# Token-major projections of 512 columns in a hybrid encoder block, two heads' pairs of keys and queries by way of DRAM

## The chip, the core and the metric

The kernel runs on one NeuronCore of a Trainium2 chip. The metric is device time in microseconds (us), lowest is best; the median of three runs stands for a kernel. One further execution was taken by the hardware profiler, and all views below come from it. Engines are called as in the profile: PE (matrix multiply; PEld is its weight load), DVE (vector), ACT (scalar, activations), POOL (GpSimd) and SP (which here only issues DMAs).

## What is computed

One layer of an encoder on 1024 tokens of 1024 channels, in float32. Cut to what matters:

```
h = rmsnorm(x);  z = h @ w_in                      # 7176 columns, split as
hq, hf, hi, hg (512 each), fq, fk, fv (512 each), ff (8), mq (512), gate_logits (3072) = split(z)
y_a = hgrn2(hq, hf, hi, hg)                        # gated recurrence, 4 heads, 128 x 128 state; hi are its values
y_b = fox(fq, fk, fv, ff)                          # 8 heads x 64, per head:
      q, k = rmsnorm(fq), rmsnorm(fk)              #   over the 64 channels of the head
      p = softmax(q k^T / 8 + F_t - F_s, causal);  y = p v
y_c = memory_attention(mq, mem)
x  = x + (sum over branches of sigmoid(gate) * (y @ w_br)) @ w_out
x  = x + (gelu(conv3(h2 @ w_a)) * (h2 @ w_v)) @ w_down,   h2 = rmsnorm(x)
```

The change touches three pieces of the first line's product: `hi`, and `fk`, `fq` of heads 4 to 7.

## The kernel before

**Three matmuls for one product.** Every float32 operand is split into a high part (rounded to the PE's fast format) and a low part (the rest). `mm3` (lines 158 to 162) multiplies high by high, high by low and low by high into one PSUM tile. A weight piece arrives by DMA in a `raw` tile (two buffers), ACT casts it into `wh` (L166), DVE subtracts to get `wl` (L174); `wh` and `wl` have three buffers each of 4 x 264 columns (`weights`, lines 188 to 198). All of this is in SBUF for `uh` and `ul`, the two parts of the normalised input, 8 chunks of 128 channels by 1024 tokens.

**Two ways to project.** `cm_chunk` (lines 200 to 217) makes a channel-major result: the weights stand in the PE, 512 tokens stream through, 2 x 8 x 3 = 48 matmuls of 512 columns for 128 channels. `token_major` (lines 704 to 715) makes a token-major one: a 128-token block of `uh`/`ul` stands in the PE, the weight columns stream. It is called with 256 columns (264 for the second half of attention's values): two weight pieces of 4 x 256, then for each of 8 token blocks 8 x 3 = 24 matmuls into one PSUM tile of the ring `pp` (three buffers), which an `evac` on ACT scales by the token's norm `rt` and copies out.

**Fill and attention.** The FoX attention (`fox_attn`, lines 901 to 972) is done in halves (p, i), pair of heads p = 0..3, head i of the pair. For each of 8 query blocks: scores on PE (L924, L925), bias and maximum on DVE (L930), exponential on ACT (L940), scaling on POOL (L942); for each two blocks transposes on PE (L953, L954), a split, products with the values (L965, L966), and a DMA to `ybd` (L971). As this chain leaves PE time over, `weave` (lines 97 to 106) emits it together with fill, and a scheduler that simulates the engines sets the order on each engine, attention's instructions with their priority moved 300 ahead. The order on each engine's queue is then fixed, DMA issues on SP included.

The fill of each half, before: `fox_proj(p + 1)` (lines 844 to 864: keys and queries of the next pair, 256 columns, 8 tiles) in (0,0), (1,0), (2,0); three gate chunks (`gates_early`, 48 matmuls of 512 columns and two results to DRAM each) in (0,1), (1,1), (2,1); eight tiles of `hgrn_values` (lines 1012 to 1016) and one gate chunk in (3,0), the other eight tiles in (3,1). `NFOX` deals the gate chunks. `fox_proj`'s evac writes tiles `z` of four token blocks (two buffers) and after each fourth block normalises them: a square on ACT (L859, into a buffer of the ring `pt`, which attention's probabilities share), a sum on DVE (L860), a power on POOL (L179), a multiplication on DVE (L862). `fox_prep(p + 1)` (lines 866 to 892) then transposes `z` on PE (L878), after the last score matmul of half (p, 0), and builds the operands of pair p + 1, which is used one half later. Behind attention comes the recurrence: `hgrn_prep` (six results of 48 / 2 matmuls a head) is its fill, `hgrn_mix` its chain.

Unrelated to that, POOL issues DMAs by software (`G.dma_start`): weights of the dense units and of the second half's channel mixer, and the sums of the down weights.

Of the kernel before, what the change touches and what calls it, by code (L numbers as in the profile page):

```python
# [8 lines left out]
F32 = mybir.dt.float32  # L9
F32R = mybir.dt.float32r  # L10
# [4 lines left out]
P = 128  # L15
T = 1024
D = 1024
KC = D // P
# [9 lines left out]
ORDER = [(br, j) for br in (1, 0, 2) for j in range(8)]  # L28
NCOVER, NPAIR = 2, 10
NDULL = 8  # L30
NFOX = [0, 3, 0, 3, 0, 3, 1]

_dense = [12, 13, 14, 15] + [16 + 8 * br + j for br, j in ORDER[4:4 + NPAIR]]
PAIRS = list(zip(_dense[0::2], _dense[1::2]))
assert 2 + NCOVER + NPAIR + sum(NFOX) == len(ORDER) and len(_dense) % 2 == 0
# [56 lines left out]
def run_all(gen):  # L92
    for _ in gen:
        pass


def weave(*parts):

    live = [[g, max(n, 1), s[0] if s else 0.0, 0] for g, n, *s in parts]
    while live:  # L100
        p = min(live, key=lambda q: q[2] + (1.0 - q[2]) * q[3] / q[1])
        try:
            next(p[0])
            p[3] += 1
        except StopIteration:
            live.remove(p)


@with_exitstack
def tile_block(ctx: ExitStack, tc: tile.TileContext, xT, memT, x_rows, mem_rows, vec, fbias, mats, hmask, w_first, w_cm, w_hi, w_fqk, w_fv,  # L110
               w_mkv, w_br, w_out, w_up, w_dn, w_pair, outT):
    nc = tc.nc
    V, S, G, PE, SP = nc.vector, nc.scalar, nc.gpsimd, nc.tensor, nc.sync
# [34 lines left out]
    def ahead(gen, offset):  # L148

        while True:  # L150
            with tc.high_priority(offset) if offset else nullcontext():
                try:
                    next(gen)
                except StopIteration:
                    return
            yield

    def mm3(ps, lh, ll, rh, rl, first, last, more=False):

        PE.matmul(ps, lh, rh, start=first, stop=False, skip_group_check=more)  # L160
        PE.matmul(ps, lh, rl, start=False, stop=False, skip_group_check=more)  # L161
        return PE.matmul(ps, ll, rh, start=False, stop=last, skip_group_check=more)  # L162
# [259 lines left out]
    def first_weights(k):  # L422
        k0, k1 = WFIRST[k]
        if k % 4 == 0:
            gw[k // 4] = [wp.tile([P, 4 * 264], F32R, tag=t, name=t, bufs=3) for t in ("wh", "wl")]
# [133 lines left out]
    class Dense:  # L559
# [15 lines left out]

        def operand(self, src):
            if self.half is None:
                self.half = [wp.tile([P, 4 * 264], F32R, tag=t, name=t, bufs=3) for t in ("wh", "wl")]
# [137 lines left out]

# [124 lines left out]
    fox_sets = {}  # L841
    fox_z = {}

    def fox_proj(p):

        fox_z[p] = [None, None]

        def evac(tb, ps):
            n, b = tb // 4, tb % 4
            if b == 0:  # L850
                fox_z[p][n] = pq.tile([P, 4, 256], F32, tag="z", name=f"z{p}_{n}", bufs=2)
            z = fox_z[p][n]
            S.activation(z[:, b, :], ps, AF.Copy, scale=rt[:, tb:tb + 1])
            if b == 3:
                zz = z.rearrange("p b (h d) -> p (b h) d", d=64)
                sq = pools["pf"].tile([P, 16, 64], F32, tag="pt", name="fsq", bufs=4) if p else \
                    pm.tile([P, 16, 64], F32, tag="fsq", name="fsq")
                r = cp.tile([P, 16], F32, tag="fr", name="fr", bufs=2)
                S.activation(sq, zz, AF.Square)  # L859
                V.reduce_sum(r, sq, axis=AX.X)  # L860
                rstd_small(r, r, 64)
                V.tensor_mul(zz, zz, r.unsqueeze(2).to_broadcast([P, 16, 64]))  # L862
# [115 lines left out]
    mskf = pf.tile([P, P], F32, tag="mskf", name="mskf")  # L978
    SP.dma_start(mskf, mats[:, 2 * P:3 * P])
    fox_prep(0)  # L980
    for p in range(3):
        weave((ahead(fox_attn(p, 0), AHEAD), FOX_STEPS), (fox_proj(p + 1), 8))
        fox_prep(p + 1, fox_sets[p][3])
        weave((ahead(fox_attn(p, 1), AHEAD), FOX_STEPS), (gates_early(NFOX[2 * p + 1]), 2 * NFOX[2 * p + 1], FOX_LATE))


    state = {}
# [22 lines left out]
        SP.dma_start(state["rs"], mats[:, 3 * P:3 * P + HB])  # L1010

    def hgrn_values():
        for pc in range(2):
            def evac(tb, ps, pc=pc):
                S.activation(Vf[:, tb, pc * 256:(pc + 1) * 256], ps, AF.Copy, scale=rt[:, tb:tb + 1])
            yield from token_major(w_hi[pc], 256, evac)

    hset = {}

# [333 lines left out]
    def first_operands():  # L1353

        raw = []
        for i in range(2):
            t = wp.tile([P, 4 * 264], F32, tag="raw", name="raw", bufs=2)
            SP.dma_start(t[:, :2 * HB], w_up[0][:, 2 * i:2 * i + 2, :])
            raw += [t[:, :HB], t[:, HB:2 * HB]]
        a11, a21, a22, a12 = raw  # L1360
        h = [wp.tile([P, 4 * 264], F32R, tag="wh", name="wh", bufs=3) for _ in range(2)]
        sums = [wp.tile([P, 4 * 264], F32R, tag="wl", name="sums", bufs=3).bitcast(F32) for _ in range(2)]
# [346 lines left out]
def _layout(inp):  # L1709
# [68 lines left out]
    o["w_hi"] = c(np.stack(pieces(hi, [(0, 256), (256, 512)])))  # L1778
    o["w_fqk"] = c(np.stack([pieces(np.concatenate([fk[:, p * P:(p + 1) * P], fq[:, p * P:(p + 1) * P]], axis=1),
                                    [(0, 256)])[0] for p in range(4)]))  # L1780
# [34 lines left out]
```

## Time and profile before

| | us |
|---|---|
| runs | 1698.50, 1698.43, 1699.84; median 1698.5 |
| the profiled execution, its own time | 1700.23 |
| its span, first to last instruction | 1698.4 |
| PE busy | 1691.0 |
| DVE, ACT, POOL busy | 1150.8, 800.9, 324.6 |
| mean granted PE clock | 0.999 |

The span is what lies between the first and the last instruction of the program on the core; the execution's own time has 1.8 us more around it. A busy time is the union of the instructions' durations on an engine, so matmuls that overlap in the PE's pipeline count once. A row of a group has the line, the engine, the operation, the names written and read, shapes and count; then busy time, the mean duration of one in ns, and the engine's idle time before them. A line is often a helper's, so names tell more: `pp<-wh,uh 128x256` is token-major, `pp<-uh,wh 128x512` channel-major.

### The profile page before, as it was taken

To read this page: it belongs to the slowest core of one execution; us is meant where nothing else is said; L and a number is where in the kernel's file an instruction comes from. 1 tells how busy PE (TensorE), PEld (TensorE's weight loads), DVE (VectorE), ACT (ScalarE), POOL (GpSimd) and SP (SyncE) were. 2 spreads that over 40 slices of the span, in tenths; PEclk is the share of its full clock that TensorE was granted. 3 is DMA by queue.
4 is the path that set the end of the run, shared out by engine and by line. 5 is a ranking of instruction groups with operands and counts; after the bars stand their busy time and mean duration, and the time that the engine had idled before them with its cause. 6 is when DMAs were issued, how large, how long until landed. Compare 5 with 4: busy or idle time off the path is not lost.

```text
span 1698.4 us, 24291 instructions
## 1 busy us (share of the span) xinstructions
PE 1691.0 (100%) x8957; PEld 1452.4 (86%) x8957; DVE 1150.8 (68%) x2057; ACT 800.9 (47%) x1428; POOL 324.6 (19%) x420
## 2 busy tenths in 40 slices
PE   9999999999999999999999999999999999999999
PEld 7888899989898998888888888888888888888887
DVE  6966455666666664886856845987878888775654
ACT  6734455545454553775631333644434444533432
POOL 0200032543433331544310000311111111100000
PEclk9999999999999999999999999999999999999999
DMA  9443232221212111110346542566544344494772
GB/s 367 157 161 106 88 139 68 77 92 51 94 59 77 63 46 57 67 32 13 106 127 209 167 186 100 165 174 169 158 139 138 118 149 143 172 363 145 251 269 87
DMA packets 83062, 227.16 MB, mean 134 GB/s; under 512 B 9712, under 2 KB 12408, under 8 KB 82816
## 3 DMA queue, kind: packets, MB, share of 16 engines
q1 hardware_dynamic: 64320, 160.54, 26.8%
q0 software_dynamic: 18048, 64.50, 13.2%
q8 instruction: 70, 1.15, 0.3%
q10 hardware_dynamic: 576, 0.59, 0.1%
q14 instruction: 48, 0.39, 0.1%
HBM read 180.72 MB, written 67.93 MB: 146 GB/s over the span
## 4 chain that ended last, share of the span: by engine, by line
PE 99%; DVE 0%; ACT 0%; DMA 0%; issue 0%; ACTq 0%; DVEq 0%
PE pp L160 21%; PE pp L162 21%; PE pp L161 21%; PE lg L160 4%; PE lg L162 4%; PE lg L161 4%; PE tr L162 3%; PE tr L161 3%; PE tr L160 3%; PE po L966 1%; PE lg L925 1%; PE lg L924 1%; PE po L965 1%; PE po L160 1%; PE po L161 1%; PE po L162 1%
## 5 line engine op out<-in xcount | busy, mean ns | idle before, releaser
L160 PE MATMUL pp<-uh,wh 128*128 128x512 f32 x412 | 163.3, 396 | 0.0
L161 PE MATMUL pp<-ul,wh 128*128 128x512 f32 x412 | 162.9, 395 | 0.0
L162 PE MATMUL pp<-uh,wl 128*128 128x512 f32 x412 | 162.5, 394 | 0.0
L161 PE MATMUL pp<-wl,uh 128*128 128x256 f32 (+1 forms) x512 | 146.3, 286 | 0.0
L162 PE MATMUL pp<-wh,ul 128*128 128x256 f32 (+1 forms) x512 | 146.1, 286 | 0.0
L160 PE MATMUL pp<-wh,uh 128*128 128x256 f32 (+1 forms) x512 | 145.6, 286 | 0.0
L166 ACT CAST wh<-s 128x512 fp32r<-128x512 f32 x110 | 66.5, 621 | 131.6 <-PE pp L161 55.1
L166 ACT CAST wh<-raw 128x1024 fp32r<-128x1024 f32 (+2 forms) x76 | 67.6, 890 | 100.6 <-PE pp L161 86.2
L166 ACT CAST wh<-rw 128x512 fp32r<-128x512 f32 x87 | 53.2, 619 | 108.1 <-PE pp L161 70.2
L160 PEld LDWEIGHTS pp<-wh,uh 128*128 128x128 f32 x512 | 97.3, 190 | 1.2
L161 PEld LDWEIGHTS pp<-wl,uh 128*128 128x128 f32 x512 | 97.4, 190 | 1.0
L162 PEld LDWEIGHTS pp<-wh,ul 128*128 128x128 f32 x512 | 97.4, 190 | 0.9
L1457 POOL DMA_DIRECT2D rw<-in_w_up x44 | 24.1, 555 | 372.4 <-DVE wl L1350 171.3
L166 ACT CAST dwh<-wr 128x1024 fp32r<-128x1024 f32 (+1 forms) x41 | 40.2, 980 | 115.8 <-PE tr L161 40.0
L162 PEld LDWEIGHTS pp<-uh,wl 128*128 128x128 f32 x412 | 77.5, 188 | 15.1
L174 DVE TENSOR_TENSOR wl<-raw,wh 128x1024 fp32r<-128x1024 f32 (+2 forms) x75 | 78.0, 1040 | 17.8 <-ACT wh L166 17.6
L160 PEld LDWEIGHTS pp<-uh,wh 128*128 128x128 f32 x412 | 77.5, 188 | 14.6
L161 PEld LDWEIGHTS pp<-ul,wh 128*128 128x128 f32 x412 | 77.5, 188 | 14.5
L940 ACT ACTIVATE pt<-pt,st 128x128 f32<-128x128 f32 (+3 forms) x64 | 49.7, 777 | 41.7 <-DVE st L937 33.9
L174 DVE TENSOR_TENSOR dwl<-wr,dwh 128x1024 fp32r<-128x1024 f32 (+1 forms) x41 | 46.3, 1129 | 31.7 <-ACT dwh L166 31.7
L942 POOL TENSOR_SCALAR pt<-pt,st 128x128 f32<-128x128 f32 (+3 forms) x64 | 49.1, 767 | 78.4 <-DVE st L941 64.1
L1350 DVE TENSOR_TENSOR wl<-rw,wh 128x512 fp32r<-128x512 f32 x69 | 47.7, 704 | 22.7 <-PE pp L162 18.2
(500 smaller groups left out, 5123.2 us busy)
## 6 DMA issues: line engine op xcount, KB each, us to landing
rw<-in_w_up POOLq DMA_DIRECT2D x44, 512.0 KB, 4.7
sd<-in_w_dn POOLq DMA_DIRECT2D x30, 512.0 KB, 6.0
br<-yd SPq DMA_DIRECT2D x30, 512.0 KB, 5.0
raw<-in_w_cm SPq DMA_DIRECT2D x24, 512.0 KB, 3.4
gd<-gt SPq DMA_DIRECT2D x48, 256.0 KB, 2.0
gt<-gd SPq DMA_DIRECT2D x48, 256.0 KB, 2.7
yd<-fc SPq DMA_DIRECT2D x44, 256.0 KB, 2.2
wr<-sd SPq DMA_DIRECT2D x20, 512.0 KB, 4.5
```

What stands on the lines that cost most here:

```text
L160: PE.matmul(ps, lh, rh, start=first, stop=False, skip_group_check=more)
L161: PE.matmul(ps, lh, rl, start=False, stop=False, skip_group_check=more)
L162: return PE.matmul(ps, ll, rh, start=False, stop=last, skip_group_check=more)
L166: return S.copy(out, in_)
L174: return (sub or V).tensor_sub(l, src, h.bitcast(F32))
L924: PE.matmul(ps[:, :w], qa[i][:, tsl], kh[i][:, s0:s0 + w], start=True, stop=False)
L925: fox_sets[p][3] = PE.matmul(ps[:, :w], qa[i][:, tsl], kl[i][:, s0:s0 + w], start=False, stop=True)
L940: S.activation(pt[:, :ns], pt[:, :ns], AF.Exp, bias=st[:, 2:3], accum_out=st[:, 3:4])
L942: G.tensor_scalar(pt[:, :ns], pt[:, :ns], st[:, 3:4], 0.0, ALU.mult, ALU.add)
L965: PE.matmul(o, vhl[:, sb, :], ph[:, src], start=(sb == 0), stop=False)
L1350: late["split"] = V.tensor_sub(l, src, h.bitcast(F32))
L1457: late["raw"] = G.dma_start(raw[:, 2 * i:2 * i + 2, :], src[:, 2 * i:2 * i + 2, :])
```

## The change

The weights of `hi`, and those of `fk`, `fq` of pairs 2 and 3 together, become two arrays of 512 columns, `w_late`, in four pieces of 2 x 512 each; `token_major` takes two 128-row chunks a piece at 512 columns, four at 256 or 264. `hgrn_values` makes 8 tiles of 512 columns in place of 16 of 256. Pairs 2 and 3 are projected by `fox_proj_late`, 8 tiles of 512 columns, which go from a gate tile to the DRAM tile `zd`; `fox_load(p)` reads a pair's 256 columns back into `z` (two DMAs of four token blocks) and normalises. `wh` and `wl` get four buffers (`WIDE`), and the SBUF scratch of the software DMAs shrinks from its default of 16384 bytes a partition to 4096. The fill is dealt thus: (0,0) `fox_proj(1)`; (0,1) a gate chunk, then four late tiles; (1,0) four late tiles, with `fox_load(2)`; (1,1) three gate chunks; (2,0) two gate chunks, with `fox_load(3)`; (2,1) three; (3,0) one, then four tiles of the recurrence's values; (3,1) the other four.

```diff
-NFOX = [0, 3, 0, 3, 0, 3, 1]
+NFOX = 10
+WIDE = 4
@@ weights(), first_weights(), Dense.operand(), first_operands()
-            hl = [wp.tile([P, 4 * 264], F32R, tag=t, name=t, bufs=3) for t in ("wh", "wl")]
+            hl = [wp.tile([P, 4 * 264], F32R, tag=t, name=t, bufs=WIDE) for t in ("wh", "wl")]
@@ token_major()
-            w = [weights(src[q], (4, ncol)) for q in range(2)]
+            per = 2 if ncol == HB else 4
+            w = [weights(src[q], (per, ncol)) for q in range(KC // per)]
...
-                wh, wl = w[k // 4]
-                mm3(ps, uh[k][:, tsl], ul[k][:, tsl], wh[:, k % 4, :], wl[:, k % 4, :], k == 0, k == KC - 1)
+                wh, wl = w[k // per]
+                mm3(ps, uh[k][:, tsl], ul[k][:, tsl], wh[:, k % per, :], wl[:, k % per, :], k == 0, k == KC - 1)
@@
+    zd = tc.dram_tile([8, P, HB], F32, name="zd")
+
+    def fox_norm(p, z):
...
+    def fox_proj_late():
+
+        def evac(tb, ps):
+            t = gate_tile()
+            S.activation(t, ps, AF.Copy, scale=rt[:, tb:tb + 1])
+            SP.dma_start(zd[tb], t)
+
+        yield from token_major(w_late[0], HB, evac)
+
+    def fox_load(p):
+        cs = slice((p - 2) * 256, (p - 1) * 256)
+        for n in range(2):
+            z = fox_tile(p, n)
+            SP.dma_start(z, zd[4 * n:4 * n + 4, :, cs].rearrange("b p c -> p b c"))
+            fox_norm(p, z)
+            yield
@@
+    late_proj = fox_proj_late()
+    first = (fox_proj(1), islice(late_proj, 4), gates_early(2))
+    second = (chain(gates_early(1), islice(late_proj, 4)), gates_early(3), gates_early(3))
     for p in range(3):
-        weave((ahead(fox_attn(p, 0), AHEAD), FOX_STEPS), (fox_proj(p + 1), 8))
+        weave((ahead(fox_attn(p, 0), AHEAD), FOX_STEPS), (first[p], (8, 4, 4)[p]),
+              *([(fox_load(p + 1), 2, 0.5)] if p else []))
         fox_prep(p + 1, fox_sets[p][3])
-        weave((ahead(fox_attn(p, 1), AHEAD), FOX_STEPS), (gates_early(NFOX[2 * p + 1]), 2 * NFOX[2 * p + 1], FOX_LATE))
+        weave((ahead(fox_attn(p, 1), AHEAD), FOX_STEPS), (second[p], 6, FOX_LATE))
+    run_all(late_proj)
@@ hgrn_values()
-        for pc in range(2):
-            def evac(tb, ps, pc=pc):
-                S.activation(Vf[:, tb, pc * 256:(pc + 1) * 256], ps, AF.Copy, scale=rt[:, tb:tb + 1])
-            yield from token_major(w_hi[pc], 256, evac)
+        def evac(tb, ps):
+            S.activation(Vf[:, tb, :], ps, AF.Copy, scale=rt[:, tb:tb + 1])
+        yield from token_major(w_late[1], HB, evac)
@@
-        weave((ahead(fox_attn(3, i), AHEAD), FOX_STEPS), (islice(values, 8), 8),
-              (gates_early(0 if i else NFOX[6]), 2 * NFOX[6], FOX_LATE))
+        weave((ahead(fox_attn(3, i), AHEAD), FOX_STEPS), (chain(gates_early(1 - i), islice(values, 4)), 6 - 2 * i))
@@
-    nc = bacc.Bacc("TRN2", target_bir_lowering=False, num_devices=1)
+    nc = bacc.Bacc("TRN2", target_bir_lowering=False, num_devices=1, dynamic_dma_scratch_size=4096)
```

`fox_norm` holds the four operations of L859 to L862, taken out of `fox_proj`'s evac; `fox_tile` allocates a `z` tile.

More of the change, by code (lines that the diff above doesn't have):

```diff
@@ L30 @@
 NDULL = 8
-NFOX = [0, 3, 0, 3, 0, 3, 1]
+NFOX = 10
 _dense = [12, 13, 14, 15] + [16 + 8 * br + j for br, j in ORDER[4:4 + NPAIR]]
 PAIRS = list(zip(_dense[0::2], _dense[1::2]))
-assert 2 + NCOVER + NPAIR + sum(NFOX) == len(ORDER) and len(_dense) % 2 == 0
+assert 2 + NCOVER + NPAIR + NFOX == len(ORDER) and len(_dense) % 2 == 0
 FOX_STEPS, HGRN_STEPS, MEM_STEPS = 28, 14, 7
@@ L109, in tile_block @@
 @with_exitstack
-def tile_block(ctx: ExitStack, tc: tile.TileContext, xT, memT, x_rows, mem_rows, vec, fbias, mats, hmask, w_first, w_cm, w_hi, w_fqk, w_fv,
+def tile_block(ctx: ExitStack, tc: tile.TileContext, xT, memT, x_rows, mem_rows, vec, fbias, mats, hmask, w_first, w_cm, w_late, w_fqk, w_fv,
                w_mkv, w_br, w_out, w_up, w_dn, w_pair, outT):
@@ L424, in first_weights @@
         if k % 4 == 0:
-            gw[k // 4] = [wp.tile([P, 4 * 264], F32R, tag=t, name=t, bufs=3) for t in ("wh", "wl")]
+            gw[k // 4] = [wp.tile([P, 4 * 264], F32R, tag=t, name=t, bufs=WIDE) for t in ("wh", "wl")]
         sl = slice((k0 % 4) * 256, (k1 - 1) % 4 * 256 + 256)
@@ L577, in operand @@
             if self.half is None:
-                self.half = [wp.tile([P, 4 * 264], F32R, tag=t, name=t, bufs=3) for t in ("wh", "wl")]
+                self.half = [wp.tile([P, 4 * 264], F32R, tag=t, name=t, bufs=WIDE) for t in ("wh", "wl")]
                 h, l = (t[:, :HB] for t in self.half)
@@ L842, in tile_block, with fox_tile @@
     fox_z = {}
+    zd = tc.dram_tile([8, P, HB], F32, name="zd")
+    def fox_norm(p, z):
+        zz = z.rearrange("p b (h d) -> p (b h) d", d=64)
+        sq = pools["pf"].tile([P, 16, 64], F32, tag="pt", name="fsq", bufs=4) if p else \
+            pm.tile([P, 16, 64], F32, tag="fsq", name="fsq")
+        r = cp.tile([P, 16], F32, tag="fr", name="fr", bufs=2)
+        S.activation(sq, zz, AF.Square)
+        V.reduce_sum(r, sq, axis=AX.X)
+        rstd_small(r, r, 64)
+        V.tensor_mul(zz, zz, r.unsqueeze(2).to_broadcast([P, 16, 64]))
+    def fox_tile(p, n):
+        fox_z.setdefault(p, {})[n] = z = pq.tile([P, 4, 256], F32, tag="z", name=f"z{p}_{n}", bufs=2)
+        return z
     def fox_proj(p):
-        fox_z[p] = [None, None]
         def evac(tb, ps):
@@ L850, in evac @@
             if b == 0:
-                fox_z[p][n] = pq.tile([P, 4, 256], F32, tag="z", name=f"z{p}_{n}", bufs=2)
+                fox_tile(p, n)
             z = fox_z[p][n]
@@ L854, in evac @@
             if b == 3:
[L855 to L862, printed above, removed]
-        yield from token_major(w_fqk[p], 256, evac)
+                fox_norm(p, z)
+        yield from token_major(w_fqk[p], 256, evac)
+    def fox_proj_late():
[9 more added lines that the diff above has]
+            SP.dma_start(z, zd[4 * n:4 * n + 4, :, cs].rearrange("b p c -> p b c"))
+            fox_norm(p, z)
+            yield
     def fox_prep(p, after=None):
@@ L1360, in first_operands @@
         a11, a21, a22, a12 = raw
-        h = [wp.tile([P, 4 * 264], F32R, tag="wh", name="wh", bufs=3) for _ in range(2)]
-        sums = [wp.tile([P, 4 * 264], F32R, tag="wl", name="sums", bufs=3).bitcast(F32) for _ in range(2)]
+        h = [wp.tile([P, 4 * 264], F32R, tag="wh", name="wh", bufs=WIDE) for _ in range(2)]
+        sums = [wp.tile([P, 4 * 264], F32R, tag="wl", name="sums", bufs=WIDE).bitcast(F32) for _ in range(2)]
         s1, s2, s4 = sums[0][:, :HB], sums[0][:, HB:2 * HB], sums[1][:, :HB]
@@ L1776, in pieces @@
         return out
-    o["w_hi"] = c(np.stack(pieces(hi, [(0, 256), (256, 512)])))
     o["w_fqk"] = c(np.stack([pieces(np.concatenate([fk[:, p * P:(p + 1) * P], fq[:, p * P:(p + 1) * P]], axis=1),
-                                    [(0, 256)])[0] for p in range(4)]))
+                                    [(0, 256)])[0] for p in range(2)]))
+    late = np.concatenate([m[:, p * P:(p + 1) * P] for p in (2, 3) for m in (fk, fq)], axis=1)
+    o["w_late"] = c(np.stack([kmaj(m).reshape(P, 4, 2 * HB).transpose(1, 0, 2) for m in (late, hi)]))
     pv = pieces(np.concatenate([fv, ff], axis=1), [(0, 256), (256, 520)])
@@ L1808 @@
     with tile.TileContext(nc, schedule_with_timeline_sim=True) as tc:
-        tile_block(tc, a["xT"], a["memT"], a["x_rows"], a["mem_rows"], a["vec"], a["fbias"], a["mats"], a["hmask"], a["w_first"], a["w_cm"], a["w_hi"], a["w_fqk"],
+        tile_block(tc, a["xT"], a["memT"], a["x_rows"], a["mem_rows"], a["vec"], a["fbias"], a["mats"], a["hmask"], a["w_first"], a["w_cm"], a["w_late"], a["w_fqk"],
                    (a["w_fv0"], a["w_fv1"]), a["w_mkv"], a["w_br"], a["w_out"], a["w_up"], a["w_dn"],
```

## The prediction

> **What bounds the kernel now.** I read the page first: the engines' busy shares, the slices and the chain that ended last.
>
> ```profile
> span 1698.4 us, 24291 instructions
> ...
> PE 1691.0 (100%) x8957; PEld 1452.4 (86%) x8957; DVE 1150.8 (68%) x2057; ACT 800.9 (47%) x1428; POOL 324.6 (19%) x420
> ...
> PEclk9999999999999999999999999999999999999999
> ...
> PE 99%; DVE 0%; ACT 0%; DMA 0%; issue 0%; ACTq 0%; DVEq 0%
> ```
>
> PE is busy in all of the span, at full clock, and 99% of the chain is PE itself. A busy PE could still be one that has fill to spare while something else sets the end, so next come the stages of the change (three stretches from pair 1's attention to the end of the recurrence) and PE's waits.
>
> ```profile
> core 0: us, PE busy (x) PEld busy (x) DVE busy (x) ACT busy (x) POOL busy (x), PEclk, DMA share, GB/s
> 431.00:564.00 133.00, 133.00 (x838) 119.38 (x837) 86.80 (x251) 69.63 (x134) 48.85 (x66) 1.00 0.21 74
> 564.00:681.00 117.00, 117.00 (x803) 108.17 (x803) 65.18 (x206) 55.88 (x113) 30.87 (x48) 1.00 0.16 53
> 681.00:890.00 209.00, 208.24 (x1201) 177.19 (x1200) 156.74 (x260) 127.14 (x304) 82.54 (x72) 1.00 0.21 68
> ```
>
> ```profile
> PE lg L160 <- ACT uh L349: 1.8, 1, 1.8
> PE tr L265 <- POOL dull L263: 1.0, 1, 1.0
> PE po L1189 <- DVE St L1195: 0.7, 1, 0.7
> PE pp L162 <- DVE wl L1350: 0.2, 1, 0.2
> ```
>
> In attention (the first two stretches) PE never stops, DVE is busy 65% and 56%, DMA engines about a fifth. Over the whole run PE waits 3.7 us, and the only wait near the change is 0.7 us in the recurrence. So PE's own instruction stream sets the time there, and a change is worth what it takes out of that stream.
>
> What a matmul costs in that stream is not its duration. These are first and last instructions of two unbroken runs of fill, with counts: 44 matmuls of 256 columns, then 76 of 512.
>
> ```profile
> 390.39 0.36 PE L160 MATMUL pp<-wh,uh 128*128 128x256 f32 x1
> 390.59 0.28 PE L161 MATMUL pp<-wl,uh 128*128 128x256 f32 x1
> ...
> 395.74 0.29 PE L162 MATMUL pp<-wh,ul 128*128 128x256 f32 x1
> ...
> 680.16 0.39 PE L162 MATMUL pp<-uh,wl 128*128 128x512 f32 x1
> ...
> 697.19 0.39 PE L162 MATMUL pp<-uh,wl 128*128 128x512 f32 x1
> ```
>
> From start to start: (395.74 - 390.59) / 43 = 0.1198 us at 256 columns, (697.19 - 680.16) / 75 = 0.2271 us at 512. The durations (0.28, 0.39) overlap; whoever subtracts them gets 2 x 0.28 - 0.39 = 0.17 us for each pair merged, fourteen times what the stream shows: 2 x 0.1198 - 0.2271 = 0.0125 us. The two points lie on 12.5 ns plus 0.419 ns a column: the change saves the constant of one matmul in two and no column.
>
> **The change part by part.**
>
> *Wider matmuls.* Removed: pairs 2 and 3 and the two halves of the recurrence's values, 4 calls of 8 tiles x 24 = 768 matmuls of 256 columns. Added: 2 calls of 8 x 24 = 384 of 512. 768 x 0.1198 = 92.0 us go, 384 x 0.2271 = 87.2 come: **-4.8 us**. They lie where PE is the bound, so the whole of it counts. The stationary operand, the same blocks of `uh` and `ul`, is loaded half as often; no transpose is added, as `z` has its old shape.
>
> A rule speaks against this term. The Trainium skill, "TensorE: Matmul & The Clock Gate", section Back-to-back issue gap, has a warm gap of N / 2.4 + 2.5 ns; by it two narrow matmuls take 218.3 ns and the wide one 215.8, and the sum would be 384 x 2.5 ns = 1.0 us, a time of 1697.5. The trace does not agree: its constant is 12.5 ns, five times as much, at a granted clock of 1.00.
>
> *Switches.* The first step of the narrow run above took 390.59 - 390.39 = 0.20 us in place of 0.12, after transposes. A new order may have some 30 more or fewer such changes between attention and fill (an estimate: about one for each of attention's 32 pairs of blocks): 30 x 0.08 = 2.4 us either way; I take 0.
>
> *Evacuation and weight splits.* The rows for these, from 390 to 681:
>
> ```profile
> L174 DVE TENSOR_TENSOR wl<-raw,wh 128x1024 fp32r<-128x1024 f32 x18 | 22.2, 1234 | 8.1 <-ACT wh L166 8.0
> ...
> L166 ACT CAST wh<-raw 128x1024 fp32r<-128x1024 f32 x17 | 17.8, 1045 | 9.2 <-PE pp L161 7.1 <-PE pp L162 2.2
> ...
> L465 ACT ACTIVATE gt<-gt 128x512 f32<-128x512 f32 x14 | 8.9, 632 | 14.3 <-DVE gt L464 14.3
> ...
> L853 ACT ACTIVATE z<-pp,rt 128x256 f32<-128x256 f32 x16 | 7.5, 471 | 7.5 <-PE pp L162 7.3
> ...
> L1015 ACT ACTIVATE Vf<-pp,rt 128x256 f32<-128x256 f32 x16 | 7.5, 473 | 5.0 <-PE pp L162 4.6
> ```
>
> 32 evacuations of 0.47 us (15.0) become 16 of some 0.63, by the 512-column row (10.1): 5 us less of ACT, which is busy half the time, so 0. The split is of 8 x 1024 columns before and after, 1.05 + 1.23 us a piece. What changes is room: two pieces of three buffers left one free for the next group, four of four leave none. At each of four joints (into and out of the late projection and the values) one piece can be cast only when the group before has freed its buffer. A tile takes its chunks in order, so a new group's last piece is needed 18 matmuls after its first tile begins, and an old group's first piece falls free 18 matmuls before its end: 18 x 0.2271 = 4.1 us of cover against 2.28 for cast and subtraction. I take 0; uncovered it is 2.28 a joint, 9.1 in all. ACT waits in such a cast, and attention's exponentials behind it wait too. For the gain side the extra buffer could end only the waits listed above, 0.2 us at most.
>
> *The way through DRAM.* Added to SP's queue: 8 writes of 256 KB and 4 reads of 512 KB. The nearest rows, with POOL's two largest and POOL's queue:
>
> ```profile
> q0 software_dynamic: 18048, 64.50, 13.2%
> ...
> rw<-in_w_up POOLq DMA_DIRECT2D x44, 512.0 KB, 4.7
> sd<-in_w_dn POOLq DMA_DIRECT2D x30, 512.0 KB, 6.0
> ...
> gd<-gt SPq DMA_DIRECT2D x48, 256.0 KB, 2.0
> ...
> sd<-sd POOLq DMA_DIRECT2D x10, 512.0 KB, 5.4
> ...
> mqf<-mqd SPq DMA_DIRECT2D x4, 512.0 KB, 4.2
> ```
>
> 2.0 + 4.2 = 6.2 us later is `z` of pair 2's second half; pair 3's lies in DRAM half a pair earlier. Behind the read that waits for the last write, SP holds weight loads, `nf`, gate results and `ybd`. Here is what hides it: pair 2's last evacuation, its last square, and the first transposes that use it.
>
> ```profile
> 423.50 0.48 ACT L853 ACTIVATE z<-pp,rt 128x256 f32<-128x256 f32 x1 [0.94 <-PE pp L162]
> ...
> 451.77 1.07 ACT L859 ACTIVATE fsq<-z 128x1024 f32<-128x1024 f32 x1 [0.78 <-PE tr L953]
> ...
> 471.41 0.84 PE L878 MATMUL tr<-ident,z 128*128 128x128 f32 x6
> ```
>
> 28 us pass from evacuation to square and 20 from there to the transposes, so 6.2 us fit. Cost 0; with the cover gone 6.2, once.
>
> *Dealing.* Fill of a half, before: 8 narrow tiles 23.0 us, or three gate chunks 3 x 48 x 0.2271 = 32.7; in (3,0) 23.0 + 10.9. After: 23.0, 32.7, 21.8, 32.7, 21.8, 32.7, 32.7, 21.8. No half differs by more than 1.2 us: 0.
>
> *Scratch.* No view shows it as a resource. Best case 0. Worst, each POOL DMA waits for the one before: 44 x 4.7 + 30 x 6.0 + 10 x 5.4 = 441 us of landing in the mixer's 22 units of 84 matmuls, 420 us: 21 us. Nearest is 0, as 64.50 MB in 18048 packets is 140 packets per 0.5 MB, on 16 engines some 9 each. The Trainium skill, "DMA: Bandwidth & Descriptors", in its terms, has 16 bytes for a descriptor, which software puts into rings in SBUF; by an estimate from that 4096 bytes hold 256, and no DMA waits. No run here shows the ring.
>
> **Sum.** The profiled execution took 1700.23 (its span 1698.4); less 4.8, 1695.4 (span 1693.6). That execution lies 1.7 above the median 1698.5 of the runs shown, so for the median I predict **1693.7**, 0.28% less.
>
> **Rivals.** About 0.2%, 3.4 us, can be told from no change here.
>
> *Absorbed by the chain.* Attention and recurrence, not PE, might set the end, fill only moving up: then 1698.5. For it: fill runs far ahead. The values' last tile is evacuated while attention has another 40 us to go (its last product comes at 679.8); the first two rows are for the next paragraph:
>
> ```profile
> 578.27 0.80 POOL L942 TENSOR_SCALAR pt<-pt,st 128x640 f32<-128x640 f32 x1 [1.69 <-DVE st L941]
> ...
> 582.21 0.27 PE L953 MATMUL tr<-ident,pt 128*128 128x128 f32 x1
> ...
> 639.07 0.47 ACT L1015 ACTIVATE Vf<-pp,rt 128x256 f32<-128x256 f32 x1
> ...
> 679.76 0.28 PE L966 MATMUL po<-pl,vhl 128*128 128x128 f32 x1
> ```
>
> Against: the chain's data wait for PE, not PE for them. The scaled probabilities of the first row are ready at 579.07 and transposed 3.1 us later. 4.8 us over 32 pairs of blocks take 0.15 from such a margin.
>
> *Columns alone.* If the constant belongs to a column's share of a tile, a wide token-major matmul takes 0.2396: no gain, 1698.5. Against: the channel-major run at 0.2271, with as many weight loads. (The skill's gap, cited above, would lead to nearly the same, 1697.5, by the other way.)
>
> *DRAM trip exposed.* 1693.7 + 6.2 = 1699.9.
>
> *Joints (slower).* Four groups that fill all buffers, each waiting 2.28 us for its last or next piece: 1693.7 + 9.1 = 1702.8. It decides when ACT and DVE come to the piece over 4.1 - 2.28 = 1.8 us late, and turns the sign once three of four joints are bare (6.8). For it: ACT's casts already wait for PE 9.2 us in 17. Against: attention's matmuls come in between and lengthen the cover.
>
> *Scratch too small.* 1693.7 + 21 = 1714.7.
>
> **How the numbers follow.** Forecast 0.64, of which 0.05 is lost below the limit by switches; absorbed 0.13, columns alone 0.02, DRAM trip 0.06, joints 0.13, scratch 0.02. Faster 0.59; same 0.05 + 0.13 + 0.02 + 0.06 = 0.26; slower 0.15. The forecast's own range is 1693.7 - 2.4 = 1691.3 to 1696.1. The range reaches up to the DRAM trip, 1700, and leaves out joints and scratch, 0.15.
>
> **What would show it.** Right: `pp<-wh,uh` splits into 256 of 256/264 and 128 of 512 for each line, wide ones at about 0.227 from start to start; PE still without waits from 390 to 870; attention's last product some 4 us sooner. Wrong: PE waiting on `wh` or `wl` (L166, L174) at a joint; L878 waiting on `z`; L942 to L953 margins shrunk to nothing and idle PE before the branches; POOL's issues late in the mixer. A wide pace of 0.24 would break the main term.

## The result, and the profile after

The changed kernel takes **1719.05 us** (median of four runs, 1717.72 to 1722.29) against 1699.17 of the kernel before on the same chip: ratio 1.0119, 95% interval 1.0102 to 1.0137. It is 20 us slower; 1693.7 was predicted, 1691.3 to 1700.0 as the range. The profiled execution took 1720.06 us, its span 1718.3, 19.9 more than the span before.

The page of the changed kernel: span, PE's row, PE in 40 slices, the chain.

```profile
span 1718.3 us, 23535 instructions
...
PE 1695.9 (99%) x8573; PEld 1434.4 (83%) x8573; DVE 1149.8 (67%) x2057; ACT 796.9 (46%) x1412; POOL 327.7 (19%) x420
...
PE   9999999999999899999999999899999999999999
...
PE 86%; issue 11%; DVE 1%; DMA 1%; ACT 1%; POOL 0%; ACTq 0%; POOLq 0%; DVEq 0%
```

PE has 384 matmuls fewer, as worked out, and two slices that are no longer full: the 14th (558 to 601 us, attention) and the 26th (1074 to 1117, start of the channel mixer). The windows of the changed kernel, all engines, show how narrow the two holes are:

```profile
core 0: us, PE busy (x) PEld busy (x) DVE busy (x) ACT busy (x) POOL busy (x), PEclk, DMA share, GB/s
382.00:575.00 193.00, 193.00 (x1017) 164.32 (x1016) 112.27 (x315) 90.65 (x166) 61.61 (x81) 1.00 0.27 96
575.00:614.00 39.00, 29.45 (x174) 23.02 (x173) 32.84 (x120) 26.03 (x55) 23.35 (x37) 0.91 0.08 25
614.00:692.00 78.00, 78.00 (x419) 66.47 (x418) 37.21 (x111) 33.28 (x64) 16.21 (x24) 1.00 0.16 54
...
1083.00:1102.00 19.00, 13.32 (x57) 9.87 (x56) 13.48 (x21) 10.07 (x19) 9.71 (x12) 0.91 0.53 170
```

*The budget.* I counted every PE instruction of both traces at its usual start-to-start time (0.227 us at 512 columns, 0.120 at 256, 0.11 for the rest) and took what is left over as lost. No view prints this; it is worked out from the instructions' starts. In attention's halves nothing is lost before and 17.1 us after; from 1075 to 1125 us 0.6 before and 8.5 after. With the shorter stream, -4.8 + 17.1 + 7.9 = 20.2 us, against 19.9 in the spans.

**First hole: attention has no fill.** These are the fill's matmuls (those that write `pp`) in attention's halves (0,1) to (3,1), each window running from one half's last product to the next one's; first the kernel before, then after. Columns: length, PE busy with fill, its matmuls.

```profile
core 0: us, PE busy (x), PEclk, DMA share, GB/s
382.40:429.30 46.90, 36.46 (x233) 1.00 0.19 63
429.30:471.10 41.80, 32.12 (x128) 1.00 0.22 76
471.10:519.10 48.00, 37.87 (x235) 1.00 0.18 61
519.10:562.50 43.40, 33.82 (x154) 1.00 0.24 86
562.50:608.80 46.30, 36.22 (x231) 1.00 0.20 63
608.80:639.30 30.50, 21.83 (x145) 1.00 0.09 27
639.30:679.80 40.50, 32.18 (x129) 1.00 0.18 60
```

```profile
381.10:440.50 59.40, 48.05 (x196) 1.00 0.31 111
440.50:487.90 47.40, 37.53 (x150) 1.00 0.26 89
487.90:545.80 57.90, 46.69 (x189) 1.00 0.30 102
545.80:581.80 36.00, 23.05 (x90) 1.00 0.14 50
581.80:609.50 27.70, 0.00 (x0) 0.88 0.09 30
609.50:650.20 40.70, 29.20 (x116) 1.00 0.09 26
650.20:690.30 40.10, 31.29 (x125) 1.00 0.23 80
```

Read the counts, not the times. The halves (0,1), (1,1), (2,1) hold about 230 fill matmuls each before, and the first two of them 196 and 189 after; (1,0) holds 128 and 150. That is not the amount dealt to them (three gate chunks would be 144). The fill runs as far ahead as the order lets it, and how far that is goes by the number of matmuls. Before, the i = 1 halves have mostly narrow ones (the first has 192 of 256 columns and 41 of 512), so 230 cost 32 us. After, all are wide, and 196 and 189 cost 44.5 and 42.9 us. The first three halves grow by 28 us and use up fill that (2,1) would have had. The recurrence's values, the last projection in the fill, begin at 549.7 us before and at 551.0 after, but attention then stands 31 us into (2,0) before and only 5 us after. In (2,1) it runs alone: 27.7 us, fill 0.

What stops the fill just there is the tile `Vf`, which holds attention's values and then takes the recurrence's. Three tiles of the recurrence's values are made by 575 us and fill the ring `pp`; their evacuations come together, once attention's values of head 7 have been split out of `Vf`:

```profile
612.61 1.85 ACT L1045 ACTIVATE Vf<-pp,rt 128x512 f32<-128x512 f32 x3 [0.23 <-DVE vhl L175]
```

Whether this wait also makes the loss is what the first two experiments ask.

The same place of head 1 in both traces, PE's timeline, from the last transposes of a pair of blocks to the next scores of 512 columns; before, then after:

```profile
400.61 0.27 PE L956 MATMUL tr<-ident,pt 128*128 128x128 f32 x1
400.64 0.36 PE L161 MATMUL pp<-wl,uh 128*128 128x256 f32 x1
...
402.73 0.28 PE L162 MATMUL pp<-wh,ul 128*128 128x256 f32 x1
402.85 0.40 PE L924 MATMUL lg<-kh,qa 128*128 128x512 f32 x1
```

```profile
404.24 0.27 PE L982 MATMUL tr<-ident,pt 128*128 128x128 f32 x1
...
404.59 0.40 PE L163 MATMUL pp<-wh,ul 128*128 128x512 f32 x1
...
408.62 0.39 PE L162 MATMUL pp<-wl,uh 128*128 128x512 f32 x1
408.85 0.39 PE L950 MATMUL lg<-kh,qa 128*128 128x512 f32 x1
```

Between them lie 17 fill matmuls before and 18 after: 2.24 us and 4.61 us. (One transpose lies between as well, and in the kernel after two score matmuls of 256 columns, at 404.27 and 404.47 us.) Over all stretches from last transposes to first products with at least four fill matmuls, single stretches differ widely (4 to 27 matmuls), but the median is 17 matmuls and 2.48 us beside narrow fill, 19 and 4.99 us beside wide fill of the kernel before (gate chunks), 19 and 5.04 us after. **PE's order has about the same number of matmuls between two steps of attention whatever their width**, so wide fill takes twice as long there. In the hole, PE waits where it never did before (`issue` means that the profile shows nothing that it waited for):

```profile
582.45 0.28 PE L951 MATMUL lg<-kl,qa 128*128 128x128 f32 x1
585.51 0.63 PE L904 MATMUL tr<-ident,z 128*128 128x128 f32 x4 [2.79 <-issue]
586.70 1.09 PE L904 MATMUL tr<-ident,z 128*128 128x128 f32 x4 [0.56 <-DVE qa L916]
590.22 0.45 PE L979 MATMUL tr<-ident,pt 128*128 128x128 f32 x1 [2.43 <-DVE kl L910]
```

**Second hole: the mixer's first weights come late.** POOL's timeline around the start of the channel mixer, before and after:

```profile
1053.27 1.06 POOL L1457 DMA_DIRECT2D rw<-in_w_up  x2 [163.03 <-ACT sqs L1392]
1068.02 1.05 POOL L1457 DMA_DIRECT2D rw<-in_w_up  x2 [13.69 <-ACT B22h L166]
1071.70 2.65 POOL L179 TENSOR_TENSOR rt<-rt,mhalf 128x8 f32<-128x8 f32 x1 [2.63 <-DVE rt L178]
```

```profile
1082.81 2.04 POOL L180 TENSOR_TENSOR rt<-rt,mhalf 128x8 f32<-128x8 f32 x1 [180.83 <-DVE rt L179]
1084.82 2.15 POOL L1486 DMA_DIRECT2D rw<-in_w_up  x4
```

Before, the loads of the first two units go out 18 and 4 us ahead of the second norm's power; after, all four stand behind it in POOL's queue. PE then waits for an operand of the first unit, and pays twice:

```profile
1093.94 0.39 PE L161 MATMUL tr<-B21h,wh 128*128 128x512 f32 x1
1098.01 0.50 PE L162 MATMUL tr<-B21l,wh 128*128 128x512 f32 x1 [3.68 <-DVE B21l L175]
...
1098.97 0.63 PE L162 MATMUL tr<-B21l,wh 128*128 128x512 f32 x1
...
1101.95 0.43 PE L163 MATMUL tr<-B21h,wl 128*128 128x512 f32 x1
```

Seven steps from 1098.97 to 1101.95 take 0.426 us each instead of 0.227, 1.4 us more.

### The profile page after: what moved, and what is told of

Its sections match the earlier page's. It is cut to its first block, busy times and chain, and to the rows that moved or that the text cites. A ratio compares the mean times of both kernels' runs of the same rounds, so it can differ in the third digit from the quotient of the medians.

```text
span 1718.3 us, 23535 instructions
## 1 busy us (share of the span) xinstructions
PE 1695.9 (99%) x8573; PEld 1434.4 (83%) x8573; DVE 1149.8 (67%) x2057; ACT 796.9 (46%) x1412; POOL 327.7 (19%) x420
## 4 chain that ended last, share of the span: by engine, by line
PE 86%; issue 11%; DVE 1%; DMA 1%; ACT 1%; POOL 0%; ACTq 0%; POOLq 0%; DVEq 0%
PE pp L161 18%; PE pp L162 18%; PE pp L163 18%; PE lg L161 4%; PE lg L163 4%; PE lg L162 4%; PE tr L162 3%; PE tr L161 3%; PE tr L163 3%; PE po L992 1%; PE po L161 1%; PE po L163 1%; PE po L162 1%; PE lg L951 1%; PE lg L950 1%
## 5 line engine op out<-in xcount | busy, mean ns | idle before, releaser
L163 PE MATMUL pp<-uh,wl 128*128 128x512 f32 x412 | 162.6, 395 | 0.0
L162 PE MATMUL pp<-wl,uh 128*128 128x256 f32 (+2 forms) x384 | 124.0, 323 | 0.0
L161 PE MATMUL pp<-wh,uh 128*128 128x256 f32 (+2 forms) x384 | 123.3, 322 | 0.0
L163 PE MATMUL pp<-wh,ul 128*128 128x256 f32 (+2 forms) x384 | 123.1, 321 | 0.0
L163 PEld LDWEIGHTS pp<-uh,wl 128*128 128x128 f32 x412 | 77.5, 188 | 15.3
L162 PEld LDWEIGHTS pp<-wl,uh 128*128 128x128 f32 x384 | 72.8, 190 | 5.1
L163 PEld LDWEIGHTS pp<-wh,ul 128*128 128x128 f32 x384 | 72.8, 190 | 4.9
L161 PEld LDWEIGHTS pp<-wh,uh 128*128 128x128 f32 x384 | 72.8, 190 | 4.8
L956 DVE CUSTOM_DVE_ANT_0 pt<-lg,nf 128x512 f32<-128x512 f32 (+2 forms) x80 | 41.4, 524 | 34.4 <-PE tr L979 17.0
```

What stands on the lines that cost most here:

```text
L956: V.tensor_tensor_reduce(out=pt[:, s0 + lo:s0 + hi], in0=ps[:, lo:hi], in1=bias, op0=ALU.add, op1=ALU.max, scale=1.0, scalar=-3e38, accum_ ...
```

## The experiments

Fourteen kernels, each beside runs of the kernel before on the same chip (its medians 1699.4 to 1700.2). Edits are against the changed kernel unless "before" is named. The first theories: A, the hole in attention is a wait for the buffer `Vf` (the 512-column values overwrite columns 256 to 511, which hold the values of heads 4 to 7, and so wait for head 7's split); D, the mixer's loss comes with the four weight buffers and their scratch.

**narrow_values**: the recurrence's values in two calls of 256 columns, as before.

```diff
-        yield from token_major(w_late[1], HB, evac)
+        for pc in range(2):
...
+            yield from token_major(w_hi[pc], 256, evac)
```

> The changed kernel, with the recurrence's values made again in two calls of 256 columns, their order of fill kept. Theory A (a wide tile's evacuation overwrites Vf's columns of heads 4 to 7, so it must wait until the last of them is split): the narrow first call overwrites heads 0 to 3 alone, the PE gap near 577 to 613 us goes, and what is left is 2.4 us won by the wide late projection and about 8 us lost at the start of the channel mixer: 1699 - 2.4 + 8.2 = 1705. Rival B (groups that fill all four weight buffers wait at their joints): two of four joints are left, half of the gap of some 15 us stays: about 1712. Rival C (z of pair 3 comes late through DRAM): unchanged, 1719, as that way is kept.

1721.94 us, 1.0129 (1.0112 to 1.0146). Half of the wait is gone: the first eight values flow at once, the second eight still wait for head 7's split (three of them are evacuated together at 621.28 us). The time does not fall, and the hole only moves (fill matmuls in (2,0), (2,1), (3,0): 194, 88, 148).

**third_vhl**: a third buffer for the split values, so that head 7 need not wait.

```diff
-        vhl = pf.tile([P, 8, P], F32R, tag="vhl", name="vhl", bufs=2)
+        vhl = pf.tile([P, 8, P], F32R, tag="vhl", name="vhl", bufs=3)
...
-    nc = bacc.Bacc("TRN2", target_bir_lowering=False, num_devices=1, dynamic_dma_scratch_size=4096)
+    nc = bacc.Bacc("TRN2", target_bir_lowering=False, num_devices=1, dynamic_dma_scratch_size=3072)
```

> The changed kernel with three buffers in place of two for vhl, the split values of one head (the software DMAs' scratch is cut to 3072 bytes to make room). Theory A: head 7 can be split when pair 2's first half is done, some 30 us earlier, so the wide values flow as fill: the gap near 577 us shrinks from 36 us to under 10, time 1699 - 4.8 + 8.2 = 1703 to 1706. Rivals B and C: nothing of theirs is changed, 1719.

1725.2 us, 1.0155 (1.014 to 1.017). A falls as the cause of the loss: the values are evacuated from 586.38 us on, 26 us sooner, and the time rises. Now (2,1) has 152 fill matmuls, part of them the recurrence's first head, and the last half has none:

```profile
583.10:637.80 54.70, 40.31 (x152) 0.94 0.18 54
637.80:676.80 39.00, 28.77 (x112) 1.00 0.14 48
676.80:698.50 21.70, 0.00 (x0) 0.84 0.13 38
```

The buffer sets where the hole falls, not that there is one.

**before_wide4**: the kernel before, with four buffers and the small scratch, nothing else.

```diff
-            hl = [wp.tile([P, 4 * 264], F32R, tag=t, name=t, bufs=3) for t in ("wh", "wl")]
+            hl = [wp.tile([P, 4 * 264], F32R, tag=t, name=t, bufs=WIDE) for t in ("wh", "wl")]
...
-    nc = bacc.Bacc("TRN2", target_bir_lowering=False, num_devices=1)
+    nc = bacc.Bacc("TRN2", target_bir_lowering=False, num_devices=1, dynamic_dma_scratch_size=4096)
```

> The kernel before with four buffers for wh and wl and a scratch of 4096 bytes, no projection changed. Theory D (the loss of 8 us at the start of the channel mixer comes of the buffers alone, as POOL's order then has the second norm's power ahead of the mixer's first weight loads): the same gap appears there, 1699 + 8 = 1707. Rival E (it comes of the changed fill, or of the shift of everything behind it): no gap, 1699.

1707.13 us, 1.0045 (1.003 to 1.006). Attention is as before; POOL has its power first and its four loads behind it, and the loss of 7.2 us lies at 1050 to 1100 us. The second hole is made by these two settings alone; which share each has, before_scratch asks.

**loads_first**: the power placed behind the mixer's first load on POOL.

```diff
-        rstd_small(rt2, ps[:, :8], D)
+        late["norm2"] = ps
...
+            with tc.issue_after(late["raw"].ins):
+                rstd_small(rt2, late["norm2"][:, :8], D)
```

> The changed kernel with the second norm's mean and power placed behind the mixer's first weight load on POOL. Theory D: the first load no longer waits for the norm, most of the 8 us at the mixer's start comes back: 1711 to 1713. If the order of POOL does not matter (rival: the operands wait for wh and wl buffers): 1719. The gap near 577 us stays under both.

1714.94 us, 1.009 (1.0075 to 1.0105), 4.1 less than after. By the count of the budget 5.3 of the second hole's 7.9 us are gone. The first unit's load goes out at 1053.0 again, the second's still after the power.

**split_columns**: all of the change stays, but each 512-column product group is made as two groups of 256.

```diff
-            for k in range(KC):
-                wh, wl = w[k // per]
-                mm3(ps, uh[k][:, tsl], ul[k][:, tsl], wh[:, k % per, :], wl[:, k % per, :], k == 0, k == KC - 1)
+            for c in range(0, ncol, 256 if ncol == HB else ncol):
+                cc = slice(c, c + (256 if ncol == HB else ncol))
+                for k in range(KC):
+                    wh, wl = w[k // per]
+                    mm3(ps[:, cc], uh[k][:, tsl], ul[k][:, tsl], wh[:, k % per, cc], wl[:, k % per, cc], k == 0, k == KC - 1)
```

> Everything of the change stays (dealing, DRAM way, wide tiles, Vf, four buffers, scratch); only each 512-column product group of the late projection and the values is made of two groups of 256 columns in the same bank, one after the other. Theory 'paced by count' (between an attention group's last transposes and its first products the order places 17 to 19 fill matmuls whatever their width, 2.48 us at 256 columns and 5.0 us at 512): the hops beside those tiles fall from 5.0 to 2.5 us, attention ends near 681 instead of 691.5, PE's idle time at 575 to 613 goes; the 4.8 us of the wide pace are given up and the 8 us at the channel mixer stay, so 1719 - 16.5 + 4.8 = 1707 us. Theory 'dealing or DRAM way or Vf': the gap stays and the time is 1719 + 4.8 = 1724 us.

1713.17 us, 1.008 (1.0062 to 1.0098): halfway between the two. With 384 matmuls more it is 5.9 us *faster* than after, so the width alone costs 5.9 + 4.8 = 10.7 us of lost PE time. By the count, some 9 of them lie in the first hole and 2 at the channel mixer, whose start is also less late here (5.7 us lost instead of 7.9); why, no run shows. Half (0,1) takes 244 matmuls in 43.6 us; but (1,1), which the new dealing gives to gate chunks, is as long as ever, and 8.0 us of the first hole stay:

```profile
375.20:418.80 43.60, 33.17 (x244) 1.00 0.19 62
418.80:463.30 44.50, 35.20 (x166) 1.00 0.37 126
463.30:524.40 61.10, 49.22 (x202) 1.00 0.33 108
```

**deal_narrow**: the new dealing and the way through DRAM, all projections at 256 columns, three buffers, the scratch of before.

```diff
-        yield from token_major(w_late[0], HB, evac)
...
+            yield from token_major(w_fqk[2 + q], 256, evac)
...
-    first = (fox_proj(1), islice(late_proj, 4), gates_early(2))
+    first = (fox_proj(1), islice(late_proj, 8), gates_early(2))
-WIDE = 4
+WIDE = 3
```

> The change's dealing and its way through DRAM with 256-column projections throughout, three buffers and the scratch of before. Theory 'paced by count': hops of 2.5 us beside the projections, attention halves of 32 to 46 us, no gap, channel mixer as before: 1697 to 1701 us. Theory 'dealing or DRAM way': the gap of 16 us at 575 to 613 stays: 1712 to 1716 us.

1712.34 us, 1.0071 (1.0053 to 1.0089). The expectation under "paced by count" was wrong: I had looked at the width of the projections only, and not at which halves the wide gate chunks are dealt to. Half (1,1):

```profile
468.30:527.00 58.70, 46.85 (x193) 1.00 0.32 104
```

193 matmuls, all of 512 columns, against 187 narrow and 48 wide ones before: 43.8 us of fill instead of 33.3. The bill comes mostly at attention's end, where the stock of fill is out: PE waits 2.2 us for the recurrence's gate tile at 687 us and 4.3 us for `kE` at 700. In attention itself the count loses only 3 us.

**before_dram**: the kernel before, with only pairs 2 and 3 sent through DRAM (dealing, widths, buffers as before).

```diff
+        def evac(tb, ps):
+            t = gate_tile()
+            S.activation(t[:, :256], ps, AF.Copy, scale=rt[:, tb:tb + 1])
+            SP.dma_start(zd[tb][:, cs], t[:, :256])
...
+            SP.dma_start(z, zd[4 * n:4 * n + 4, :, cs].rearrange("b p c -> p b c"))
```

> Before with only the way of pairs 2 and 3 through DRAM (256-column projections, dealing, buffers and scratch of before). The order on PE has the same fill in each half within 5 us. If the way through DRAM costs nothing, 1699 us (1697 to 1701); if the loaded tiles come late at the joints, 1703 to 1706 us.

1700.57 us, 1.0005 (0.9995 to 1.0014): the way through DRAM costs nothing that can be measured. What deal_narrow lost, 11 to 12 us, is the dealing's.

**more_fill**: one pair of gate chunks fewer by the method of differences, two more chunks (21.8 us) as fill.

```diff
-NCOVER, NPAIR = 2, 10
+NCOVER, NPAIR = 2, 8
...
-NFOX = 10
+NFOX = 12
...
-    first = (fox_proj(1), islice(late_proj, 4), gates_early(2))
-    second = (chain(gates_early(1), islice(late_proj, 4)), gates_early(3), gates_early(3))
+    first = (fox_proj(1), islice(late_proj, 4), gates_early(3))
+    second = (chain(gates_early(1), islice(late_proj, 4)), gates_early(3), gates_early(4))
```

> After with one pair of gate chunks fewer by differences (8 instead of 10) and these two chunks dealt as fill of attention (21.8 us of PE more). The differences' eighth is lost (2.7 us). Theory 'the fill runs out before attention does': the gap of 16.5 us shrinks by about its whole, 1719 - 16.5 + 2.7 = 1705 us, attention still at 47 to 60 us a half. If the gap were a wait for a buffer (Vf) it stays and only moves: 1719 to 1722 us.

1717.35 us, 1.0104 (1.0088 to 1.012); 1705 was expected. The chunks are taken where the order has room for matmuls, mostly in (2,0) (149 instead of 90); (2,1) has 38. Of 17.1 us lost 12.5 remain. More stock helps little while each of the first halves takes 140 to 195 wide matmuls.

**late_split_loads**: late projection at 256 columns, values at 512, and the edit of loads_first.

```diff
-        yield from token_major(w_late[0], HB, evac)
+        yield from token_major(w_late[0], HB, evac, 256)
```

> Late projection in 256-column groups, values at 512, and the second norm's power after the mixer's first loads on POOL. 'Paced by count': halves (0,1) and (1,0) back to 42 to 48 us, the gap gone or under 5 us, 2.4 us of the wide pace kept, 4 us left at the mixer: 1700 to 1704 us. Other theories: 1715 + 2.4 = 1717 us.

1710.7 us, 1.0064 (1.0048 to 1.008). Not the 1700 to 1704 hoped for: the dealing's share stays, as in split_columns.

**paced** and **paced_loads**: each step of the fill may only be placed on PE behind the attention matmul six steps back; the second with loads_first's edit.

```diff
+    def paced(gen):
+
+        while True:
+            with tc.issue_after(at_fox[-6].ins) if len(at_fox) >= 6 else nullcontext():
...
+                at_fox.append(prod)
...
-        weave((ahead(fox_attn(p, 1), AHEAD), FOX_STEPS), (second[p], 6, FOX_LATE))
+        weave((ahead(fox_attn(p, 1), AHEAD), FOX_STEPS), (paced(second[p]), 6, FOX_LATE))
```

> After with wide tiles, DRAM way, dealing and buffers as they are; each step of attention's fill may only be placed on PE behind the attention matmul six steps back, so that no half can take more fill than is dealt to it. Theory 'paced by count' (the order puts so many fill matmuls between attention's steps whatever they cost; 512 columns at twice the time stretch halves 1 to 3 by 27 us and empty the stock): each half takes 25 to 30 us of fill, no half without fill, attention ends near 640 to 680 us, the 16.5 us of idle PE are gone: 1719 - 16.5 = 1702.5 us (1700 to 1705), the mixer's 8 us remaining. If the idle time comes from the DRAM way, Vf or the wide tiles as such, it stays: 1715 to 1725 us.

> The paced fill and the power placed behind the mixer's first loads together. If the two sites are independent, 1702.5 - 4 = 1698.5 us (1696.5 to 1701), level with the kernel before: the 4.8 us of the wide pace against 4 us left at the mixer.

1742.57 us, 1.025 (1.0235 to 1.0266), and 1740.61 us, 1.0242 (1.0225 to 1.0259). Both missed by 40 us. Fill per half is even as meant (25 to 30 us after the first), but PE waits at the joints of the pairs, for `z` and for the new pair's operands, which free-running fill had covered; PE's waits in attention, paced:

```profile
PE tr L991 <- DVE kl L910: 7.5, 3, 3.1
PE tr L904 <- DVE z L856: 6.8, 2, 3.6
PE lg L961 <- DVE st L967: 4.6, 2, 4.3
```

**paced_far** and **paced_far_loads**: 22 steps back instead of 6; the second also issues both first raw loads of the mixer ahead of the power.

```diff
+            with tc.issue_after(at_fox[-22].ins) if len(at_fox) >= 22 else nullcontext():
...
+            late["next"] = load(w_up[1])
...
+            with tc.issue_after(late["raw"].ins):
+                rstd_small(rt2, late["norm2"][:, :8], D)
```

> After with the fill allowed to run 22 attention steps ahead (more than one half of 18) instead of 6. By the order of the program each half then has 25 to 32 us of fill (39 in the first), the joints of the pairs keep theirs, and no half is without. Theory 'fill spent too early, by count': idle time of attention falls from 17 to under 5 us, 1719 - 13 = 1706 us (1702 to 1708), attention's end at 676 to 682 us. If the joints need the free fill of after, idle time as in the paced run: 1715 us or more.

> The same, and at the channel mixer both first raw loads are issued on POOL before the second norm's power. If the mixer's loss is the order on POOL alone, its 8 us go too: 1706 - 8 = 1698 us (1695 to 1701). If the loads wait longer because the fourth buffer lies where they land, 3 us or more stay: 1701 us or more.

1723.21 us, 1.0133 (1.0118 to 1.0148), and 1718.23 us, 1.0111 (1.0094 to 1.0127). The long wait at (2,1) is gone, and as much is lost in (0,1) to (1,1), 7.1, 3.8 and 8.0 us by the count above, at granted clocks of 0.94, 0.96 and 0.93. So an even sum per half is not enough. My reading is that within a half the fill comes in lumps of whole tiles; no run tests it. At the mixer, in paced_far_loads, both loads now lie ahead of the power, but the second waits until 1084.6 for a product (releaser PE, L163), and 3.2 us are still lost, about as many as in loads_first, where it stands behind the power. So POOL's order makes some 5 of the 8 us; the rest goes with a load that waits for a product's operands, as the releaser has it.

**before_scratch**: the kernel before with the small scratch and three buffers.

```diff
-    nc = bacc.Bacc("TRN2", target_bir_lowering=False, num_devices=1)
+    nc = bacc.Bacc("TRN2", target_bir_lowering=False, num_devices=1, dynamic_dma_scratch_size=4096)
```

> Before with nothing but the smaller DMA scratch. If the fourth weight buffer alone makes the loss at the mixer, 1699 us as before; if the scratch has a share in it, up to 1707 us (the run of before with four buffers and this scratch).

1711.13 us, 1.0067 (1.0052 to 1.0082), a loss I did not expect, in a third place: one wait of 8.3 us at 904 us, when PE goes from the recurrence to the branches. Its waits there and SP's timeline:

```profile
DVE gt L1293 <- DMA gt<-gd: 11.4, 2, 10.6
...
PE pp L160 <- DVE gt L1293: 8.3, 1, 8.3
```

```profile
892.80 7.14 SPq L1336 DMA_DIRECT2D x<-in_xT  x8
902.29 0.33 SPq L1286 DMA_DIRECT2D gt<-gd  x1
```

Eight loads of 512 KB of the residual stand in SP's queue ahead of the gate load that the next branch needs (in the kernel before, that stretch of the queue holds gates and branch weights only, and the eight follow at 977 us). The gate load pays twice: it is issued 5 us later than before (902.29 us instead of 897.33), and beside those 4 MB it takes 9.3 us to land instead of 5.0. POOL's DMAs at the mixer come in the old order. With four buffers beside it the same scratch loses nothing here and 7 us there. My reading is that the map of SBUF changes, and with it when a tile's place is free and which load may go first; the runs show only the orders.

## Why the prediction was wrong

The step that failed is **Dealing**, "No half differs by more than 1.2 us: 0". It counted what is dealt to a half, but a half does not consume what is dealt to it. It consumes as many matmuls as the order has between attention's steps, in (0,1) to (1,1) of the two kernels some 190 to 235 with i = 1 and some 130 to 150 with i = 0, and their width sets what that costs. Measured: 11 to 12 us for the dealing alone (deal_narrow against before_dram), 10.7 us for the width alone (split_columns against after), of which some 9 in the first hole; dealing and width overlap in the 17 us of that hole, since both empty the same stock.

That dealing, width, and buffers with scratch make the loss is shown by taking them one at a time. That the count of matmuls is the way in which the first two do it fits the counts of every half, but it did not forecast: split_columns, deal_narrow, more_fill, late_split_loads, paced and paced_far all came out slower than it said, by 6 to 40 us, and no run holds the count and the placing apart.

*Absorbed by the chain* was put aside by "4.8 us over 32 pairs take 0.15 from such a margin". That spread the change of the whole over the whole. The margin of 3.1 us that I read between scaling and transposes was no reserve of time: it was what the order had placed between them, with seven fill matmuls of 512 columns among it, 1.6 us of the 3.1.

*Wider matmuls*, -4.8: right in pace (from 405.63 to 408.62 us in the changed kernel, 13 steps of 0.230 us; the median of all neighbouring wide token-major matmuls is 0.227) and in count (8573 instead of 8957). The gain was real, and lost time of five times its size (17.1 + 7.9 us) came against it.

*Switches*, 0: right. In (0,1) to (1,1), where fill never stops, the count loses 0.7 us after and nothing before.

*Evacuation and weight splits*: the joints cost 0 as said; PE waits for no `wh` or `wl` in attention. But "the extra buffer could end only the waits listed, 0.2 us at most" looked only for what the buffer gives. Together with the scratch it took 7.2 us at a place 400 us later (before_wide4), which no rival named: "joints" and "scratch too small", which held the chances for a slower kernel, are waits that did not come.

*Scratch*, 0: right that no DMA waits for the one before (the four loads at 1084.82 us are issued within 2.15 us, and the first lands only after 4.1), wrong as a sum. Alone it cost 11 us (before_scratch), by a queue's order.

*The way through DRAM*, 0: right, 0.6 us with an interval that holds 0.

Of the signs listed, two came: "POOL's issues late in the mixer", and PE idle; but the idle time lay in attention, 80 to 110 us ahead of attention's end.

None of the kernels run here beats the one before. What stays open is why the order counts matmuls and not their time, and whether an order that weighs wide fill twice would keep the 4.8 us; neither was tried.

## What to carry to other kernels

Where a fixed order weaves a latency chain with fill, count the fill instructions between two steps of the chain and multiply by what each takes; if the count doesn't follow the width, a wider instruction is a slower chain. Fill is a stock: ask whether it lasts to the chain's end, half by half, before asking what it saves. A buffer count or a scratch size is an edit of every later load too: compare each DMA queue's order with that of before, far from the place that the change is about.

## What had not been expected of the hardware

A stop of PE costs more than its length. After 4.1 us from start to start at the mixer, PE took 0.426 us for each 512-column step for 3 us, at a granted clock of 0.50 (1098.6 to 1102.0 us). The Trainium skill, "TensorE: Matmul & The Clock Gate", Part 1: The HAM clock gate, says that PE falls to half its clock after an idle window of about 3.4 us and returns after a busy one of that length; at 1.2 GHz 512 columns would be 426.7 ns by its figures, and the trace agrees to a nanosecond. On the length of the stop the traces differ. In attention's hole the granted clock is 0.50 from 586.6 to 593.4 us, 1.1 us behind a stop of 2.8 us (0.88 over the whole half); in before_wide4 it is 0.50 from 1085.0 to 1088.4, behind a stop of 2.4 us. At the mixer of loads_first it stays at 1.00 through a stop of 1.9 us; at that of paced_loads it falls to 0.50 behind one of 1.8. So stops shorter than 3.4 us were followed by a halved clock, and these runs show no length below which a stop is safe.
